# Pinning the gathered-row steps of a retrieval layer between the one-hots of its gate map

## The chip, the cores and the metric

The kernel runs on one core of a Trainium2 chip. The metric is device time in microseconds (us) of one launch, the median of several runs. The core's engines work through their own instruction lists in order: PE (matrix multiply), DVE (vector), ACT (activation), POOL (here the engine that issues gathers) and SP (here the engine that issues the other DMAs). An engine that waits for another one, or for a DMA, holds up everything behind it in its own list.

## The reference, cut to what matters

One decoder layer over 528 tokens: a mixing sub-layer (state-space scan and convolution), then the retrieval sub-layer that the change touches, then a final norm. The retrieval, per token:

```python
s1, s2 = q1 . sub_keys_1, q2 . sub_keys_2          # 8 heads, 128 scores each
v1, i1 = top_k(s1, 16);  v2, i2 = top_k(s2, 16)    # first top-k
top_s, pos = top_k(v1[:, None] + v2[None, :], 16)  # second top-k, over the 16*16 sums
expert = i1 * 128 + i2 at pos;  gate = softmax(top_s)
y = sum over 128 (head, k): gate * gelu(x . w_down[expert]) * w_up[expert]
```

There are 16384 experts with rows of 1024 float32 in `w_down` and in `w_up`. The input has 512 tokens that are kept.

## The kernel before, in words

The 512 tokens are four tiles of 128. Three of them are computed densely: all 16384 experts are multiplied with the 384 tokens, 128 experts at a time, and a gate map (a 128 x 128 table for each token, nonzero at its chosen experts) selects. The fourth tile is computed sparsely: for each of its 128 (head, k) pairs, one indirect DMA fetches 128 rows of `w_down` (512 KB), a DVE instruction multiplies them with the tokens and sums (L911), and the same is done with rows of `w_up` (L918, which adds gate times row to the output tile). That makes 256 steps, each a gather on POOL (L895) and a **use** on DVE (L911 or L918). They come out of a generator, 32 of `w_down`, then 32 of `w_up`, and so on. `pump(x)` adds x to a counter and takes as many steps as the counter's whole part.

The stages around the change, in the order of the program:

- `second(t)`, for the tiles 3, 0, 1, 2: the second top-k on DVE (many small instructions, lines 759 to 876). Tile 3 comes first, since the gathers need its expert numbers.
- `gate_map(n, b)`, 12 calls of 4 one-hot groups: each group builds four f16 one-hot tables of 128 x 1024 on DVE (L946, L947 and twice L949), 16 small matmuls on PE (L954, L955) combine them, and ACT copies the result out (L957). The one-hot tables are double-buffered.
- 86 **downs** `down(i, ...)`: 24 matmuls each (L160, L161, L162) of a 128-expert block of `w_down` with the 384 tokens. Each needs its weights split into two parts: ACT takes the high part (L754), DVE the low part (L755), and the third matmul of each triple (L162) reads what L755 wrote. There are 4 buffers for the parts. The downs are written after the map in the code, but with a higher priority (`early(AHP)`), so the build lays them between the second top-k and the map on all engines.
- The main loop over 128 blocks of `w_up`, 18 matmuls of 512 columns each, and from block 88 on with one more down in each pass. Here a use stands in each pass, later three.

The order on each engine is fixed when the kernel is built, by priorities and by an estimate of when things are ready. Gathers always keep their order of the program; a use keeps its place among the instructions that are written around it only where the list `paced` is not empty:

```python
    def use(r):
        if paced:
            tc.keep_in_program_order(r)
```

Before the main loop, gathered rows go to two buffers (`gat1`), so a gather waits on POOL until the use two steps earlier has ended. The main loop has six (`gat2`).

Of the kernel before, what the change touches and what calls it, by code (L numbers as in the profile page):

```python
# [35 lines left out]
LNP = 500  # L36
AHP = 1000
SPL = 0
SPRATE = (4.0, 1.03, 3.33, 0)
NQ = 2  # L40
NT = 4
HOLD = 2
# [75 lines left out]
def body(ctx, tc, I, out):  # L118
# [9 lines left out]
    def ps(tag="pb"):  # L128
        return psp.tile([128, 512], F32, name=tag, tag=tag)
# [4 lines left out]
    def late(n):  # L134
        return tc.high_priority(offset=-n)
# [17 lines left out]
    def load(dst, src):  # L153
        return nc.sync.dma_start(dst, src)
# [4 lines left out]
    def mm3(o, lh, ll, rh, rl, first, last):  # L159
        E.matmul(o, lh, rh, start=first, stop=False)  # L160
        E.matmul(o, lh, rl, start=False, stop=False)  # L161
        E.matmul(o, ll, rh, start=False, stop=last)  # L162
# [606 lines left out]
    def down(i, tag, ahead, leng):  # L769
        wh, wl = split_n(raw_n(I["wdT"][i].rearrange("p c j -> p (c j)"), 1024), 1024, leng)  # L770
        p = ps(tag)
        for dc in range(8):
            o = dc * 128
            mm3(p[:, :ND], wh[:, o:o + 128], wl[:, o:o + 128], hl(dc)[0][:, :ND], hl(dc)[1][:, :ND], dc == 0, dc == 7)
        hg = HG[hgn[0] % 6]
        hgn[0] += 1
        S.activation(hg, p[:, :ND], AF.Gelu)  # L777
        if ahead:
            load(HD[i], hg)
        else:  # L780
            HB[i] = hg
# [119 lines left out]
    paced = []  # L901
# [22 lines left out]
    def pump(x):  # L924
        spn[0] += x
        while spn[0] >= 1:
            spn[0] -= 1
            next(sp, None)

    for t in (3, 0, 1, 2):  # L930
        second(t)
        if t < 3:
            pump(SPRATE[3])

# [3 lines left out]
    def gate_map(n, b):  # L938
        gb = GBUF[n % 2]
        half = lambda a: a.rearrange("p t (j s) -> p t j s", s=2)  # L940
        io = iota16.rearrange("p (j s) -> p j s", s=2)[:, None].to_broadcast([128, TB, 64, 2])
        for q in range(GB // TB):
            t0 = GB * b + TB * q
            ob, oa = OB[q % 2], OA[q % 2]
            col = lambda a: a[:, t0:t0 + TB, None, :].to_broadcast([128, TB, 64, 2])
            V.tensor_tensor(half(ob), io, col(i2d), op=OP.is_equal)  # L946
            V.tensor_tensor(half(OE), io, col(i1d), op=OP.is_equal)  # L947
            for s in range(2):
                V.tensor_tensor(half(oa[s]), half(OE), col(gd[s]), op=OP.mult)  # L949
            for k0 in range(0, TB, 4):  # L950
                p = ps()
                for k in range(4):
                    po = p[:, 128 * k:128 * k + 128]
                    E.matmul(po, ob[:, k0 + k, :], oa[0][:, k0 + k, :], start=True, stop=False)  # L954
                    E.matmul(po, ob[:, k0 + k, :], oa[1][:, k0 + k, :], start=False, stop=True)  # L955
                c = TB * q + k0
                S.activation(gb.rearrange("p i t -> p t i")[:, c:c + 4, :], p.rearrange("p (t i) -> p t i", t=4),  # L957
                             AF.Copy, scale=1.0 / GS)
        for q in range(4 if n < NB - 2 else 0):
            load(GD[b, :, 32 * q:32 * q + 32, :], gb[:, 32 * q:32 * q + 32, :])  # L960

# [3 lines left out]
    def up_prep(i, leng):  # L965
        wh, wl = split_n(raw_n(I["wu"][128 * i:128 * i + 128, :], 1024), 1024, leng)
        if i not in HB:
            HB[i] = HG[hgn[0] % 6]
            hgn[0] += 1
            load(HB[i], HD[i])  # L970
        if i % 4 == 0:
            grt[i // 4] = GR[(i // 4) % 2]
            load(grt[i // 4], GD[:, :, i:i + 4, :].rearrange("b j i t -> j b i t"))
        gr = grt[i // 4]
        sf, sh, sl = SF[i % 2], SH[i % 2], SL[i % 2]
        if i >= 130 - NT:
            sh, sl = memr(R_U + 768 * (i % 2), 384), memr(R_U + 768 * (i % 2) + 384, 384)
        sf3, hb3 = [a.rearrange("p (b t) -> p b t", t=GB) for a in (sf, HB[i])]
        V.tensor_tensor(sf3[:, :NB - 2], hb3[:, :NB - 2], gr[:, :, i % 4, :], op=OP.mult)
        V.tensor_tensor(sf3[:, NB - 2:], hb3[:, NB - 2:], GLAST[:, :, GB * i:GB * i + GB], op=OP.mult)  # L980
        S.activation(sh, sf, AF.Copy)  # L981
        V.tensor_tensor(sl, sf, sh.bitcast(F32), op=OP.subtract)  # L982
        return sh, sl, wh, wl

    def up_mm(i, Y, ops, ms, hfs=(0, 1)):
        sh, sl, wh, wl = ops
        f, l = i == 0, i == 127
        for m in ms:
            c = slice(128 * m, 128 * m + 128)
            for hf in hfs:  # L990
                d = slice(512 * hf, 512 * hf + 512)
                mm3(Y[m][hf], sh[:, c], sl[:, c], wh[:, d], wl[:, d], f, l)

    for n in range(NB):
        gate_map(n, n if n < NB - 2 else 2 * NB - 3 - n)
        with late(SPL):
            pump(SPRATE[0])

    with early(AHP):
        for i in range(NQ, NAHEAD):  # L1000
# [1 line left out]

    ring[0] = gat2
    gn[0] = 0
    paced.append(True)
    ops = {}
    Y = [[ps("pa"), ps("pa")], [ps("pa"), ps("pa")], [ps(), ps()]]
    for i in range(128):
        for j in {127 - NT: range(128 - NT, 128)}.get(i, () if i > 127 - NT else (i + 1,)):
            if NAHEAD <= j < 128:  # L1010
                down(j, "pb", False, V)
        pump(0 if i < HOLD else SPRATE[1] if i < NAHEAD else SPRATE[2])
        ops[i] = up_prep(i, V)
# [48 lines left out]
```

## Time and profile before

| what | value |
|---|---|
| median of 3 runs | 1705.93 us (1703.87 to 1708.15) |
| the profiled execution: its own time, its span | 1709.63 us, 1707.9 us |
| PE busy, share of the span | 1643.6 us, 96% |
| DVE busy | 1397.6 us, 82% |
| ACT, POOL busy | 770.7 us, 397.6 us |
| second top-k with gathers, map and downs | about 637 to 1014 us |
| main loop | about 1014 to 1697 us |

The span is what the trace covers; all places below are us from its start. Busy time says how long an engine worked, not whether that work sets the end; for this one reads in a stretch which engine had idle time and whom it waited for.

### The profile page before, as it was taken

To read this page: it belongs to the slowest core of one execution; us is meant where nothing else is said; L and a number is where in the kernel's file an instruction comes from. 1 tells how busy PE (TensorE), PEld (TensorE's weight loads), DVE (VectorE), ACT (ScalarE), POOL (GpSimd) and SP (SyncE) were. 2 spreads that over 40 slices of the span, in tenths; PEclk is the share of its full clock that TensorE was granted. 3 is DMA by queue.
4 is the path that set the end of the run, shared out by engine and by line. 5 is a ranking of instruction groups with operands and counts; after the bars stand their busy time and mean duration, and the time that the engine had idled before them with its cause. 6 is when DMAs were issued, how large, how long until landed. Compare 5 with 4: busy or idle time off the path is not lost. (4 is left out here: it accounts for less than half of the span.)

```text
span 1707.9 us, 26157 instructions
## 1 busy us (share of the span) xinstructions
PE 1643.6 (96%) x9529; PEld 1487.2 (87%) x9529; DVE 1397.6 (82%) x2864; ACT 770.7 (45%) x1155; POOL 397.6 (23%) x336
## 2 busy tenths in 40 slices
PE   7999999799899999899999999999999999999997
PEld 7999999577788999898889988888888899999996
DVE  4998999974469998989889458888888889888885
ACT  5566554445333344356668533333333333333333
POOL 1111110110000003233410013222222254454540
PEclk9999999589999999999999999999999999999999
DMA  6877574454422458799888679999999899999892
GB/s 209 194 176 164 143 163 123 141 136 119 128 83 75 131 177 271 271 301 327 306 308 301 211 233 364 347 348 357 352 341 355 317 341 363 357 347 348 324 328 86
DMA packets 165185, 425.38 MB, mean 249 GB/s; under 512 B 14384, under 2 KB 81200, under 8 KB 159424
## 3 DMA queue, kind: packets, MB, share of 16 engines
q1 hardware_dynamic: 121568, 261.17, 43.8%
q0 software_dynamic: 43488, 162.55, 31.4%
q8 instruction: 74, 1.21, 0.3%
q14 instruction: 55, 0.45, 0.1%
HBM read 381.72 MB, written 41.94 MB: 248 GB/s over the span
## 5 line engine op out<-in xcount | busy, mean ns | idle before, releaser
L161 PE MATMUL pa<-MR 128*128 128x512 f32 (+3 forms) x2120 | 731.3, 345 | 3.4 <-DMA MR<-wout 3.4
L160 PE MATMUL pa<-MR 128*128 128x512 f32 (+3 forms) x2120 | 728.5, 345 | 6.1 <-ACT M L777 1.7
L162 PE MATMUL pa<-MR 128*128 128x512 f32 (+3 forms) x2120 | 693.8, 345 | 6.5 <-DVE MR L755 5.1
L160 PEld LDWEIGHTS pa<-MR 128*128 128x128 f32 x2120 | 405.2, 191 | 38.6 <-ACT M L777 2.3
L162 PEld LDWEIGHTS pa<-MR 128*128 128x128 f32 x2120 | 404.0, 191 | 38.3 <-DVE MR L755 5.4
L161 PEld LDWEIGHTS pa<-MR 128*128 128x128 f32 x2120 | 404.9, 191 | 34.9 <-DMA MR<-wout 4.6
L754 ACT ACTIVATE MR<-M 128x1024 fp32r<-128x1024 f32 (+1 forms) x264 | 285.8, 1083 | 307.1 <-PE pa L161 130.4
L755 DVE TENSOR_TENSOR MR<-M,MR 128x1024 fp32r<-128x1024 f32 (+1 forms) x264 | 330.0, 1251 | 97.4 <-ACT MR L754 96.5
L895 POOL DMA_INDIRECT M<-wu,M x128 | 177.7, 1388 | 387.4 <-DVE M L918 255.6
L895 POOL DMA_INDIRECT M<-wd,M x128 | 156.2, 1220 | 471.8 <-DVE M L911 209.6
L161 PE MATMUL pb<-MR 128*128 128x384 f32 (+1 forms) x576 | 206.6, 359 | 0.0
L160 PE MATMUL pb<-MR 128*128 128x384 f32 (+1 forms) x576 | 206.6, 359 | 0.0
L162 PE MATMUL pb<-MR 128*128 128x384 f32 (+1 forms) x576 | 205.0, 359 | 0.0
L981 ACT ACTIVATE MR<-M 128x384 fp32r<-128x384 f32 x128 | 67.0, 523 | 262.2 <-issue 202.9
L918 DVE SCALAR_TENSOR_TENSOR M<-M 128x1024 f32<-128x1024 f32 x128 | 163.5, 1278 | 15.4 <-DMA M<-wu,M 15.1
L422 DVE SCALAR_TENSOR_TENSOR M<-M 128x512 f32<-128x512 f32 x240 | 173.6, 743 | 2.6 <-ACT M L420 1.5
L911 DVE SCALAR_TENSOR_TENSOR M<-M 128x1024 f32<-128x1024 f32 x128 | 154.6, 1218 | 14.0 <-DMA M<-wd,M 13.7
L160 PEld LDWEIGHTS pb<-MR 128*128 128x128 f32 x576 | 108.1, 188 | 11.3
L161 PEld LDWEIGHTS pb<-MR 128*128 128x128 f32 x576 | 108.1, 188 | 11.2
L982 DVE TENSOR_TENSOR MR<-M,MR 128x384 fp32r<-128x384 f32 x128 | 71.0, 555 | 56.6 <-ACT MR L981 56.6
L162 PEld LDWEIGHTS pb<-MR 128*128 128x128 f32 x576 | 108.1, 188 | 10.4
L957 ACT ACTIVATE M<-pb 128x512 f32<-128x512 f32 x96 | 97.3, 1151 | 36.8 <-PE pb L955 35.2
(221 smaller groups left out, 1485.4 us busy)
## 6 DMA issues: line engine op xcount, KB each, us to landing
M<-wdT SPq DMA_DIRECT2D x128, 512.0 KB, 5.1
M<-wu SPq DMA_DIRECT2D x128, 512.0 KB, 6.5
GD<-M SPq DMA_DIRECT2D x40, 512.0 KB, 6.3
M<-GD SPq DMA_DIRECT2D x32, 640.0 KB, 7.6
M<-win SPq DMA_DIRECT2D x19, 1024.0 KB, 5.5
MR<-win POOLq DMA_DIRECT2D x38, 512.0 KB, 6.7
HD<-M SPq DMA_DIRECT2D x88, 192.0 KB, 4.3
M<-HD SPq DMA_DIRECT2D x88, 192.0 KB, 6.2
```

The source lines that it names most:

```text
L160: E.matmul(o, lh, rh, start=first, stop=False)
L161: E.matmul(o, lh, rl, start=False, stop=False)
L162: E.matmul(o, ll, rh, start=False, stop=last)
L422: V.scalar_tensor_tensor(o, gl[:, j:j + 512], cw[:, j:j + 1], o, op0=OP.mult, op1=OP.add)
L754: S.activation(wh, raw, AF.Copy)
L755: leng.tensor_tensor(wl, raw, wh.bitcast(F32), op=OP.subtract)
L895: r = G.indirect_dma_start(out=g, out_offset=None, in_=src, in_offset=bass.IndirectOffsetOnAxis(ap=e3[:, k:k + 1], axis=0))
L911: use(V.scalar_tensor_tensor(g, g, 1.0, x2s, op0=OP.mult, op1=OP.mult, accum_out=dots[:, k:k + 1]))
L918: use(V.scalar_tensor_tensor(h1[3], g, act3[:, k:k + 1], h1[3], op0=OP.mult, op1=OP.add))
L957: S.activation(gb.rearrange("p i t -> p t i")[:, c:c + 4, :], p.rearrange("p (t i) -> p t i", t=4), AF.Copy, scale=1.0 / GS)
L981: S.activation(sh, sf, AF.Copy)
L982: V.tensor_tensor(sl, sf, sh.bitcast(F32), op=OP.subtract)
```

## The change

Four numbers and three lines change. Before, four steps are pumped behind each of the 12 gate maps and their uses are not pinned. After, two steps are pumped behind the second top-k of each of the tiles 0, 1 and 2 (6, not pinned), three quarters of a step behind each of the 48 one-hot groups (36, pinned), and 6 behind the last gate map (pinned). Both make 48 steps ahead of the main loop. In the main loop a pass takes 1.0 step in place of 1.03 up to block 87, and 3.3 in place of 3.33 from there on.

```diff
-SPRATE = (4.0, 1.03, 3.33, 0)
+SPRATE = (3.0, 1.0, 3.3, 2, 6)
@@ in gate_map, in the loop over the 4 one-hot groups
                 S.activation(gb.rearrange("p i t -> p t i")[:, c:c + 4, :], p.rearrange("p (t i) -> p t i", t=4),
                              AF.Copy, scale=1.0 / GS)
+            pump(SPRATE[0] / 4)
@@ ahead of the main loop
+    paced.append(True)
     for n in range(NB):
         gate_map(n, n if n < NB - 2 else 2 * NB - 3 - n)
-        with late(SPL):
-            pump(SPRATE[0])
+    pump(SPRATE[4])
...
     ring[0] = gat2
     gn[0] = 0
-    paced.append(True)
```

The line that pumps behind a second top-k (`if t < 3: pump(SPRATE[3])`) is there before, with 0.

What this does to the order on DVE shows at three places. In the rows, L755 is the split for a down, L911 and L918 are uses, L946, L947 and L949 one-hots, the other lines small steps of the second top-k; "x2" means two in a row.

The first place is DVE in the second top-k, two rows behind the split for a down that the trace of before shows at 665.41 (rows 6). Before:

```order
L859 TENSOR_SCALAR M<-M 128x128
L911 SCALAR_TENSOR_TENSOR M<-M 128x1024
L860 TENSOR_TENSOR M<-M 128x256
L861 SCALAR_TENSOR_TENSOR M<-M 128x128
L832 TENSOR_TENSOR M<-M 128x2048
L755 TENSOR_TENSOR MR<-M,MR 128x1024
L911 SCALAR_TENSOR_TENSOR M<-M 128x1024
L834 TENSOR_TENSOR M<-M 128x2048
L862 TENSOR_SCALAR M<-M 128x128
L867 TENSOR_TENSOR M<-M 128x128
```

The same place after:

```order
L859 TENSOR_SCALAR M<-M 128x128
L860 TENSOR_TENSOR M<-M 128x256
L861 SCALAR_TENSOR_TENSOR M<-M 128x128
L832 TENSOR_TENSOR M<-M 128x2048
L834 TENSOR_TENSOR M<-M 128x2048
L755 TENSOR_TENSOR MR<-M,MR 128x1024
L862 TENSOR_SCALAR M<-M 128x128
L867 TENSOR_TENSOR M<-M 128x128
L838 TENSOR_TENSOR M<-M 128x1024
L947 TENSOR_TENSOR M<-M 128x1024
```

The uses are gone from here: from the split at 665.41 to the third split behind it (at 691.87 in rows 6) five uses stood before and none stands after, with the same steps of the second top-k between (but for one L873 and one L762, which now stand behind that split).

The second place is DVE in the midst of the map. Before:

```order
L918 SCALAR_TENSOR_TENSOR M<-M 128x1024
L947 TENSOR_TENSOR M<-M 128x1024
L755 TENSOR_TENSOR MR<-M,MR 128x1024
L949 TENSOR_TENSOR M<-M 128x1024 x2
L946 TENSOR_TENSOR M<-M 128x1024
L918 SCALAR_TENSOR_TENSOR M<-M 128x1024
L947 TENSOR_TENSOR M<-M 128x1024
L755 TENSOR_TENSOR MR<-M,MR 128x1024
L918 SCALAR_TENSOR_TENSOR M<-M 128x1024
```

After:

```order
L911 SCALAR_TENSOR_TENSOR M<-M 128x1024
L755 TENSOR_TENSOR MR<-M,MR 128x1024
L947 TENSOR_TENSOR M<-M 128x1024
L946 TENSOR_TENSOR M<-M 128x1024 x2
L949 TENSOR_TENSOR M<-M 128x1024 x2
L911 SCALAR_TENSOR_TENSOR M<-M 128x1024
L947 TENSOR_TENSOR M<-M 128x1024
L755 TENSOR_TENSOR MR<-M,MR 128x1024
L949 TENSOR_TENSOR M<-M 128x1024 x2
L911 SCALAR_TENSOR_TENSOR M<-M 128x1024
```

Here the uses now stand one behind each one-hot group, with a group between any two of them, and every fourth group has none; before, their distances are uneven. Both pieces run from one use to the second one behind it, which is the pair that shares a buffer.

The third place is DVE behind the last one-hots of the map. Before:

```order
L949 TENSOR_TENSOR M<-M 128x1024 x2
L755 TENSOR_TENSOR MR<-M,MR 128x1024 x10
L979 TENSOR_TENSOR M<-M 128x320
L980 TENSOR_TENSOR M<-M 128x64
L982 TENSOR_TENSOR MR<-M,MR 128x384
```

After (line numbers behind the map are one higher):

```order
L949 TENSOR_TENSOR M<-M 128x1024 x2
L918 SCALAR_TENSOR_TENSOR M<-M 128x1024
L755 TENSOR_TENSOR MR<-M,MR 128x1024
L918 SCALAR_TENSOR_TENSOR M<-M 128x1024
L755 TENSOR_TENSOR MR<-M,MR 128x1024
L918 SCALAR_TENSOR_TENSOR M<-M 128x1024
L755 TENSOR_TENSOR MR<-M,MR 128x1024
L918 SCALAR_TENSOR_TENSOR M<-M 128x1024 x2
L755 TENSOR_TENSOR MR<-M,MR 128x1024
L918 SCALAR_TENSOR_TENSOR M<-M 128x1024
L755 TENSOR_TENSOR MR<-M,MR 128x1024
L918 SCALAR_TENSOR_TENSOR M<-M 128x1024
```

Behind these follow seven more L755. Seven uses have come in between the last splits, where before there was none.

## Rows read from the trace of the kernel before

**Rows 1.** Page, part 1: busy us, share of the span, instructions.

```profile
PE 1643.6 (96%) x9529; PEld 1487.2 (87%) x9529; DVE 1397.6 (82%) x2864; ACT 770.7 (45%) x1155; POOL 397.6 (23%) x336
```

**Rows 2.** Waits of PE, 680 to 1000: total us, times, longest.

```profile
PE pb L954 <- DVE M L949: 8.3, 8, 2.5
PE pa L162 <- DVE MR L755: 5.1, 1, 5.1
PE pb L955 <- DVE M L949: 0.3, 1, 0.3
PE pa L160 <- ACT M L777: 0.3, 1, 0.3
```

**Rows 3.** Windows: length, then busy us of PE, PEld, DVE, ACT, POOL; PEclk, DMA share, GB/s.

```profile
697.00:699.00 2.00, 2.00 (x13) 2.00 (x12) 2.00 (x8) 0.00 (x0) 1.29 (x1) 0.92 0.98 350
836.00:838.00 2.00, 2.00 (x14) 1.84 (x13) 2.00 (x3) 2.00 (x4) 0.00 (x0) 0.68 0.77 283
```

**Rows 4.** Windows of 40 us: ahead of the main loop, and in it.

```profile
960.00:1000.00 40.00, 40.00 (x231) 39.74 (x230) 14.52 (x17) 15.10 (x22) 0.00 (x0) 1.00 0.65 215
1040.00:1080.00 40.00, 40.00 (x178) 33.12 (x177) 33.46 (x52) 14.75 (x20) 9.22 (x10) 1.00 1.01 366
```

**Rows 5.** Timeline of PE: start, duration, then idle before and its releaser.

```profile
654.96 0.33 PE L160 MATMUL pa<-MR 128*128 128x384 f32 x1
...
659.12 0.33 PE L160 MATMUL pa<-MR 128*128 128x384 f32 x1
...
693.17 0.69 PE L162 MATMUL pa<-MR 128*128 128x384 f32 x1 [5.12 <-DVE MR L755]
```

**Rows 6.** Timeline of DVE in the second top-k.

```profile
665.41 1.22 DVE L755 TENSOR_TENSOR MR<-M,MR 128x1024 fp32r<-128x1024 f32 x1
...
672.35 1.23 DVE L911 SCALAR_TENSOR_TENSOR M<-M 128x1024 f32<-128x1024 f32 x1 [0.99 <-DMA M<-wd,M]
...
691.87 1.25 DVE L755 TENSOR_TENSOR MR<-M,MR 128x1024 fp32r<-128x1024 f32 x1
```

**Rows 7.** Timeline of DVE in the map.

```profile
817.13 1.28 DVE L949 TENSOR_TENSOR M<-M 128x1024 f16<-128x1024 f16 x2
...
818.94 1.27 DVE L918 SCALAR_TENSOR_TENSOR M<-M 128x1024 f32<-128x1024 f32 x1
...
820.74 1.21 DVE L755 TENSOR_TENSOR MR<-M,MR 128x1024 fp32r<-128x1024 f32 x1
821.87 1.28 DVE L949 TENSOR_TENSOR M<-M 128x1024 f16<-128x1024 f16 x2
...
832.03 1.28 DVE L918 SCALAR_TENSOR_TENSOR M<-M 128x1024 f32<-128x1024 f32 x1 [5.34 <-DMA M<-wu,M]
...
856.96 1.28 DVE L918 SCALAR_TENSOR_TENSOR M<-M 128x1024 f32<-128x1024 f32 x1 [4.56 <-DMA M<-wu,M]
...
875.43 1.28 DVE L918 SCALAR_TENSOR_TENSOR M<-M 128x1024 f32<-128x1024 f32 x1 [2.84 <-DMA M<-wu,M]
```

**Rows 8.** Waits of DVE, 760 to 880, and of PE, 797 to 882.

```profile
DVE M L918 <- DMA M<-wu,M: 15.1, 6, 5.3
...
PE pb L954 <- DVE M L949: 6.2, 6, 2.5
```

**Rows 9.** Timeline of POOL: two gathers.

```profile
652.70 0.94 POOL L895 DMA_INDIRECT M<-wd,M  x1 [2.56 <-DVE M L911]
...
820.48 4.09 POOL L895 DMA_INDIRECT M<-wu,M  x1 [0.65 <-DVE M L918]
```

**Rows 10.** Gathers' issues, 760 to 880 and 880 to 960: median us to landing.

```profile
M<-wu,M POOLq DMA_INDIRECT x19, 8.1
...
M<-wu,M POOLq DMA_INDIRECT x3, 5.9
```

**Rows 11.** Timeline of DVE near the end of the main loop.

```profile
1675.19 1.23 DVE L755 TENSOR_TENSOR MR<-M,MR 128x1024 fp32r<-128x1024 f32 x1 [2.04 <-ACT MR L754]
...
1682.83 0.56 DVE L982 TENSOR_TENSOR MR<-M,MR 128x384 fp32r<-128x384 f32 x1 [2.31 <-ACT MR L981]
```

## The prediction, made blind

> **What bounds the kernel now.** Start with the busy times on the page: PE works for 96% of the span, DVE for 82% [rows 1]. So PE is the first candidate, and what a change can gain is what PE does not work. In the main loop it has nothing to give: in a window there PE is busy for all of its 40.00 us while DVE has 33.46 [rows 4], and so it goes on until PE's last matmul. Time that is saved or lost ahead of the main loop therefore reaches the end one for one.
>
> The change moves instructions between 637 and 1014 us, so the next view is whom PE waits for there. Four rows hold nearly all of it [rows 2]: one wait of 5.1 us for a split (L755), eight waits of 8.3 us in all and one of 0.3 for one-hots (L949), and 0.3 for ACT. DVE is thus the engine that is waited for, although it isn't the busiest. The waits cost twice where they are long, since PE runs at half clock for a while behind them. Behind the one that ended at 693.17 [rows 5] the granted clock is at its lower level of 1.2 GHz until about 697.3 (the mean of 0.92 in the stretch from 697 means 0.3 us of it at half [rows 3]): 4.1 us at half, so 2.1 lost. Behind the one at 834.0 it lasts until about 837.3 (0.68 in the stretch from 836 means 1.3 us at half): 3.3 us, so 1.6 lost. All that PE loses here is 5.1 + 0.3 + 2.1 = 7.5 us in the second top-k, and 8.3 + 0.3 + 1.6 = 10.2 in the map, 17.7 in all. That is the ceiling of a gain; work itself isn't removed on any engine.
>
> **The first place, the second top-k.** PE's wait of 5.12 us ended when the split that starts at 691.87 was done [rows 5, 6]. Five uses stand on DVE between the split at 665.41 and that one; after, none does. A use takes 1.23 us, 0.08 of it beside its successor (so 1.15), and one of the five waited 0.99 for its rows [rows 6]. The split comes 5 x 1.15 + 1.0 = 6.7 us sooner, and PE wants it 5.1 sooner. ACT's part of that down is done long before, so nothing else is late next. I count the whole 7.5 us; the bound from below is 0, if other steps of the top-k were as late.
>
> **The second place, the map.** The uses that left the second top-k now stand in the map, so DVE gets more to do there: 36 pinned uses instead of those 24 or so that the build had put into the first two thirds. What made PE wait in the map before is not DVE's work but its waiting: uses waited 15.1 us for their rows, six times [rows 8], 12.7 of it at 832.03, 856.96 and 875.43 [rows 7]. Behind a waiting use stand the one-hots that PE wants next. A gather can only start when the use two steps earlier has ended, so what counts is how much other work DVE has between a use and the second use behind it. I add it from the two excerpts of the order with steps of 1.13 us for a split, 0.60 for a one-hot and 1.20 for a use [rows 7]. Before, up to the use at 832.03: 0.60 + 1.13 + 1.20 + 0.60 + 1.20 + 0.60 + 1.13 = 6.5 us; up to the other two, added in the same way, 7.1 and 5.9. After, in the excerpt: 1.13 + 0.60 + 1.20 + 1.20 + 1.15 + 0.60 + 1.13 + 1.20 = 8.2 us. That is the close pair; two pairs of three have a further group in them and come to 10.6 or more.
>
> A gather lands 8.1 us after its issue (the median in the old map [rows 10]), and the issue comes 0.3 us behind the use's end (818.94 + 1.27 to 820.48 [rows 7, 9]): 8.4 us, just what the close pair has. The late ones still wait. If the gathers came as late as those that waited, the three long waits shrink at the close pairs by the added distance: 5.3 - 1.7 = 3.6, 4.6 - 1.1 = 3.5, 2.8 - 2.3 = 0.5, and the short ones (2.4 us in three) vanish: 7.6 us in 16 uses. Twelve uses of the 36 are such: 5.7 us. At the other 24, with 10.6, the long ones leave 1.2 + 1.1 = 2.3 in 16 uses: 3.4 us. DVE would wait some 9 us in the whole map. Of DVE's 15.1 before, PE felt 6.2 [rows 8], that is 0.41, since a finished group lies ready for it; so PE loses 9 x 0.41 = 3.7, and I take 4. The bounds are 0 (every gather at the median) and 36 x 6.2 / 16 = 14 (the old rate of waits at every use).
>
> One thing in the rows speaks against the change: a gather occupied POOL for 0.94 us beside a float32 split, and 4.09 beside f16 one-hots, a split and a use, and that gather was the one that landed at 832.03, 11.55 us after its issue [rows 7, 9]. The Trainium skill (SBUF — State Buffer, section "SBUF: two separate sides") says that DVE in a two-port mode holds the port pair that it shares with GpSimd, which then can't write the descriptors of its DMAs, so that the transfer seems blocked by DVE. By that rule the change would be bad at its core, since it puts all of the map's gathers next to one-hots; the trace agrees for the long gathers. Whatever the cause, the second rival below gives the time if all were so.
>
> **The third place, behind the map.** Seven uses now stand among the last splits, with only 2.3 to 5.3 us of work between a use and the second behind it, so they go at the pace of the gathers: two per landing and use. Landing takes 5.9 us there [rows 10] with 0.3 ahead of it, plus a use of 1.2: 7.4 for two, 26 us for seven. In that time DVE delivers five splits. PE takes 4.16 us for a down (654.96 to 659.12 [rows 5]), 6.25 downs, and with four buffers two to three splits lie ready. So I count nothing; DVE has the room later (14.52 us busy in 40 [rows 4]). Without that cover, at 11.8 us per landing, the seven take 45 us, PE could do 10.9 downs and has 7.5: 14 us lost. That is the other bound.
>
> **The rest.** In the main loop a use less in 33 passes, and 122 instead of 119.4 steps from block 88 on: the last use moves from pass 36 to pass 37 of those, one pass later. DVE has waits of 2.04 and 2.31 us there [rows 11] against one or two uses of 1.2, so nothing; up to 2 if they should not cover it. No DMA is added on SP, and the gathers pass nothing else on POOL.
>
> **The sum.** -7.5 - 10.2 + 4 = -13.7 us. The profiled execution took 1709.63 us with a span of 1707.9, so it would come to 1695.9 with a span of 1694.2. The median of the runs lies 3.7 below the profiled one, at 1705.93; the same step from there gives **1692.2 us**.
>
> **The rivals.** First, *the waits only move*: pinned uses wait for their rows at the old rate, 14 us lost in the map against 17.7 won, so -3.7: 1702. For it speaks that DVE has no less to do in all; against it the 8.2 us and more where 5.9 to 7.1 stood. Second, on the other side, *every gather in the map is as late as the one at 832.03*: 11.55 + 0.3 = 11.8 us. A gate map has one pair of 8.2 and two of 10.6: waits of 3.6 + 1.2 + 1.2 = 6.0, times 12 is 72 us on DVE, 0.41 of it 30 us on PE; 17.7 - 30 makes it 12 slower: 1718. It decides from the point where PE loses more than 17.7, that is 3.6 us of waits in a gate map, a landing 11.0 us behind a use. The median of 8.4 speaks against it; that the change sets every gather beside one-hots speaks for it. Third, *the seven uses starve PE*: +14 on the forecast, 1706, no change; the free DMA time there (0.65 of it used [rows 4]) speaks against it.
>
> **How the numbers follow.** From what a measurement of this kernel can tell, 0.3% (5.1 us), faster means under 1700.8. I give the forecast 0.70, the waits that only move 0.14, the third rival 0.08, the second 0.08. The forecast is faster, and a few of the first rival's cases too (0.02): faster 0.72. The rest of the first and most of the third are the same: 0.19. Slower: 0.09, the second and the worst of the third. The range begins at 1687, the whole 17.7 with a bit more of other waits, and ends at 1702, where the first rival lies; the others are left out. The forecast's own range is 1687 to 1698.
>
> **What would show it.** Right: PE doesn't wait at 688, the clock stays up there; PE's waits for one-hots sum to some 4 us instead of 8.6, DVE's for gathered rows in the map to under 12; PE has no wait between the last one-hot and the main loop; the main loop starts near 1000 instead of 1014. Wrong: gathers in the map that hold POOL for 3 to 4 us as a rule and land 11 us later; a wait of PE for a split behind the map; or idle time of PE in the main loop, which would mean that the saved time is lost later.

## The result, and the profile after

The changed kernel takes 1686.45 us (median of 4 runs, 1680.03 to 1686.92) against 1706.58 of the kernel before in the same comparison: a ratio of 0.9875, 95% interval 0.9848 to 0.9902. It is faster by 20.1 us; the forecast was 13.7, and the median lies 0.6 us below the low end of the range. The profiled execution has a time of 1686.24 us and a span of 1684.5.

The page of the kernel after, part 1 (against [rows 1]):

```profile
PE 1631.6 (97%) x9529; PEld 1477.1 (88%) x9529; DVE 1397.3 (83%) x2864; ACT 770.3 (46%) x1155; POOL 388.9 (23%) x336
```

No engine lost an instruction. PE has 12 us less of "busy" for the same work: 5.1 of it between the first gather and the main loop (345.4 and 340.2 us busy there), where the lower clock is gone, and 7.0 ahead of the first gather, where both kernels do the same. Whom PE waits for in the kernel after, from 640 to 1000 us (against [rows 2]):

```profile
engine line waited for: us in total, times, longest us
PE pb L880 <- DVE M L840: 1.9, 1, 1.9
PE pa L160 <- ACT M L777: 1.4, 1, 1.4
```

The wait of 5.1 us for a split in the second top-k and all nine waits for one-hots are gone. (L880 is a transpose of the second top-k, whose wait was 0.7 before; the one for L777, at 990.50, stands in the main loop.) Windows of the kernel after, the two short ones at the places of [rows 3] and the long one in the main loop as in [rows 4]; the columns are length, busy us of PE, PEld, DVE, ACT, POOL, then PE's granted clock, DMA share, GB/s:

```profile
697.00:699.00 2.00, 2.00 (x14) 2.00 (x13) 2.00 (x6) 1.17 (x3) 0.00 (x0) 1.00 0.98 258
836.00:838.00 2.00, 2.00 (x24) 1.84 (x22) 1.97 (x4) 1.43 (x2) 0.00 (x0) 1.00 1.01 414
...
1040.00:1080.00 40.00, 40.00 (x179) 33.10 (x178) 33.13 (x57) 14.75 (x20) 9.12 (x10) 1.00 0.98 356
```

The granted clock stays at its upper level where it was 0.92 and 0.68, and the main loop is as full of PE as before. So the gain lies ahead of the main loop. To measure it free of what happens earlier, take the time from the first gather to the first matmul of 512 columns, the first one of the main loop. (A few downs still stand behind it; the 1014 us given above as the start of the main loop is where those end, and after the change that is 990.5.) The two rows of the kernel before (timelines of POOL and of PE):

```profile
637.04 1.08 POOL L895 DMA_INDIRECT M<-wd,M  x1 [173.41 <-DVE M L876]
...
997.36 0.63 PE L160 MATMUL pb<-MR 128*128 128x512 f32 x2
```

and of the kernel after:

```profile
631.75 1.08 POOL L895 DMA_INDIRECT M<-wd,M  x1 [174.47 <-DVE M L876]
...
973.84 0.63 PE L160 MATMUL pb<-MR 128*128 128x512 f32 x2
```

This **stretch** is 997.36 - 637.04 = 360.3 us before and 342.1 after: 18.2 us. The gain is the same by the other mark (1014.02 - 637.04 against 990.50 - 631.75), and from the first 512-column matmul to PE's last one both kernels take 701.4 to 701.5 us. Every experiment below is read by the stretch. It is a fair measure only where it holds the same work: in four of the experiments (the added work in both forms, four at once with four buffers, nineteen uses) it holds 29 to 39 more of the downs' matmuls than the 1667 of the others, because the order at its end moved. The first gather's own start moved by 5.3 us too, but every instruction ahead of it stands in the same order in both kernels, and in the fourteen traces of this study it lies between 627 and 637 us whatever the kernel. That is scatter of the earlier stages; it is one reason why medians of a few runs differ by some us, and why the stretch is the better measure where its work is the same.

DVE's waits in the kernel after, from 700 to 910 us (in the map) and from 910 to 1000 (behind it), first rows of each:

```profile
DVE M L911 <- DMA M<-wd,M: 6.6, 6, 1.9
DVE M L918 <- DMA M<-wu,M: 2.8, 2, 1.7
```

```profile
DVE MR L755 <- ACT MR L754: 19.7, 7, 5.4
DVE M L918 <- DMA M<-wu,M: 11.6, 6, 2.6
```

DVE still waits 9.4 us for gathered rows in the map, where the forecast had 9, and 11.6 behind it. PE has no wait for one-hots or for a split beside either. Of the signs that the prediction named for being right, all came but two sizes: PE's waits for one-hots sum to 0 and not 4 us, and the main loop starts at 990.5 and not near 1000. That is the point to explain.

### The profile page after: what moved, and what is told of

It reads as the page before. It is cut to its first block, busy times and chain, and to the rows that moved or that the text cites. A ratio compares the mean times of both kernels' runs of the same rounds, so it can differ in the third digit from the quotient of the medians.

```text
span 1684.5 us, 26131 instructions
## 1 busy us (share of the span) xinstructions
PE 1631.6 (97%) x9529; PEld 1477.1 (88%) x9529; DVE 1397.3 (83%) x2864; ACT 770.3 (46%) x1155; POOL 388.9 (23%) x336
## 5 line engine op out<-in xcount | busy, mean ns | idle before, releaser
L755 DVE TENSOR_TENSOR MR<-M,MR 128x1024 fp32r<-128x1024 f32 (+1 forms) x264 | 330.5, 1253 | 81.5 <-ACT MR L754 77.1
L895 POOL DMA_INDIRECT M<-wu,M x128 | 167.2, 1306 | 310.6 <-DVE M L918 264.6
L982 ACT ACTIVATE MR<-M 128x384 fp32r<-128x384 f32 x128 | 67.0, 524 | 274.2 <-issue 203.2
L918 DVE SCALAR_TENSOR_TENSOR M<-M 128x1024 f32<-128x1024 f32 x128 | 163.8, 1279 | 14.6 <-DMA M<-wu,M 14.4
L911 DVE SCALAR_TENSOR_TENSOR M<-M 128x1024 f32<-128x1024 f32 x128 | 154.2, 1219 | 11.9 <-DMA M<-wd,M 11.9
L160 PEld LDWEIGHTS pb<-MR 128*128 128x128 f32 x576 | 108.1, 188 | 11.4
```

The lines of the kernel that those rows point to most:

```text
L755: leng.tensor_tensor(wl, raw, wh.bitcast(F32), op=OP.subtract)
L895: r = G.indirect_dma_start(out=g, out_offset=None, in_=src, in_offset=bass.IndirectOffsetOnAxis(ap=e3[:, k:k + 1], axis=0))
L911: use(V.scalar_tensor_tensor(g, g, 1.0, x2s, op0=OP.mult, op1=OP.mult, accum_out=dots[:, k:k + 1]))
L918: use(V.scalar_tensor_tensor(h1[3], g, act3[:, k:k + 1], h1[3], op0=OP.mult, op1=OP.add))
```

## The experiments

All names of lines are those of the kernel after; the stretch is worked out as above from each kernel's own two rows.

**The pin alone taken away.** The new numbers, but uses not pinned before the main loop.

```diff
-    paced.append(True)
     for n in range(NB):
         gate_map(n, n if n < NB - 2 else 2 * NB - 3 - n)
     pump(SPRATE[4])
...
+    paced.append(True)
```

> The pumps stand where the change puts them, but uses are pinned only from the main loop on, as before. The build then lays 24 uses into the second top-k and 24 into the first half of the map again, as before. My theory (pinning moves the uses, and their place is what PE loses by): the time of before, 1704 to 1708 us, with PE waiting about 5 us for a split near 688 and about 8.6 us for one-hots. Rival (the gain comes from the pumps' places in the code or from the main loop's rates of 1.0 and 3.3): near 1686.

1707.13 us, ratio 1.0015 (0.9999 to 1.0032), stretch 361.7. The build lays the uses exactly as before, and PE's waits are back:

```profile
PE pb L954 <- DVE M L949: 7.5, 7, 2.5
PE pa L162 <- DVE MR L755: 5.3, 1, 5.3
```

So the new numbers do nothing without the order that the pin fixes.

**The second top-k filled again.** Eight steps behind each of three second top-k calls in place of two, fewer in the map (24 uses and 17, in place of 7 and 34), all of the map's still pinned.

```diff
-SPRATE = (3.0, 1.0, 3.3, 2, 6)
+SPRATE = (1.5, 1.0, 3.3, 8, 6)
```

> Rates 1.5, 1.0, 3.3, 8, 6: 24 uses in the second top-k and the first one-hots as before, but only 17 in the rest of the map, 17 us of DVE work apart, 7 behind it. My theory (the two places cost separately): the top-k costs its 7.5 us again and the map nothing, so 1692 to 1696, with PE's wait of about 5 us for a split and none for one-hots. Rival (all of the gain comes from the map): 1686. Rival (all of it from the top-k): 1700 or more.

1698.71 us, ratio 0.9951 (0.9932 to 0.9969), stretch 354.6: above the 1692 to 1696 of my theory. PE's waits from 640 to 1000, and two windows, in the top-k and in the map:

```profile
PE pa L162 <- DVE MR L755: 6.1, 1, 6.1
PE pb L880 <- DVE M L840: 4.0, 3, 2.8
...
680.00:720.00 40.00, 33.54 (x182) 32.83 (x181) 37.62 (x115) 13.89 (x20) 10.15 (x10) 0.91 0.83 275
...
800.00:840.00 40.00, 40.00 (x333) 37.60 (x332) 37.52 (x55) 29.88 (x37) 7.15 (x4) 1.00 0.89 318
```

This separates the two places in one direction. With uses in the top-k, the wait for the split and the lower clock return there, and nowhere else. Of the 18.2 us, 12.5 are lost again, more than the 7.5 that the prediction gave this place, because this order has more of the L880 waits as well, with 3.4 us at the lower clock behind the longest of them; the map, which has half as many uses here as after the change, has no wait for one-hots. The other direction, an empty top-k with the long waits back in the map, was not run.

**One use behind every group.** All steps into the map: two uses ahead of it, 42 in it.

```diff
-SPRATE = (3.0, 1.0, 3.3, 2, 6)
+SPRATE = (4.0, 1.0, 3.3, 0, 0)
```

> Rates 4.0, 1.0, 3.3, 0, 0: none in the top-k, one pinned use behind each one-hot group, 48 in all, 4 of them behind the last. Pairs have 6 to 11 us of DVE work between them, much as in the changed kernel, but DVE's work in a gate map grows from 17.0 to 18.2 us against 17.7 of PE. My theory (PE feels waits for rows only where DVE has no slack left): PE waits for one-hots again, 5 to 20 us, so 1691 to 1706. Rival (number and waits do not reach PE as long as no pair is close): 1685 to 1688.

1683.88 us, ratio 0.9875 (0.9849 to 0.9902), stretch 340.6. PE has no wait at all in the stretch. My theory, that PE waits again once DVE has more work in a gate map than PE, fell: DVE's waits for rows from 700 to 910 sum to 0.9 us, and PE's for one-hots to nothing.

**Three buffers.** The kernel after with three buffers for gathered rows in the map, so that a gather can start one use earlier.

```diff
+    ring[0] = gat2[:3]
+    gn[0] = 0
     for n in range(NB):
         gate_map(n, n if n < NB - 2 else 2 * NB - 3 - n)
```

> The changed kernel with three buffers for gathered rows from the map on, so a gather starts one use earlier. DVE's waits for rows in the map (9.3 us in the changed kernel) and behind it (11.6) should vanish. My theory (PE does not feel these waits): no change, 1685 to 1688. Rival (0.4 of DVE's waits reach PE, as in my prediction): 3 to 4 us faster, 1682 to 1683.

1681.84 us, ratio 0.9870 (0.9849 to 0.9891), stretch 340.4. DVE's waits for rows from 700 to 910 are gone altogether, and the stretch is 1.7 us shorter than in the kernel after, in which the one wait for L840 alone is 1.9. Taking away the 9.4 us of waits gave PE nothing in the map, where it had no wait to lose. The median is 4.6 us below that of the kernel after, which is the rival's number and not the theory's; but the intervals of the two ratios lie over each other, and the trace shows 1.7 us of it in the stretch, none in the map.

**The change once more, and both variants together** (four steps per gate map and three buffers), in five rounds:

```diff
-SPRATE = (3.0, 1.0, 3.3, 2, 6)
+SPRATE = (4.0, 1.0, 3.3, 0, 0)
...
+    ring[0] = gat2[:3]
+    gn[0] = 0
```

> The changed kernel itself once more, in five rounds beside the kernel before. Theory: all that the change gains lies between the first gather and the main loop, where the traces show 360.3 us before and 342.1 after, so 18.2 us and a ratio near 0.989, and what stood beyond that in the first comparison (20 us, 0.9875) is the scatter of the stage ahead of it, which is the same code in both. Rival: the change also gains 2 us or more ahead of the first gather or in the main loop, and the ratio stays at 0.9875 or below.

> Three buffers and a use behind every group together, in five rounds. Both alone took PE's last wait (1.9 us for a down's input) out of the second top-k and came to 340.4 and 340.6 us between the first gather and the main loop, against 342.1 of the changed kernel; PE has nothing left to lose there, so together they give the same 340.5, and 1 to 2 us less than the changed kernel. Rival: uses land sooner still and DVE's room shows elsewhere: 4 us or more below the changed kernel.

The change: 1686.31 us, ratio 0.9882 (0.9861 to 0.9903), stretch 340.8. Both: 1684.53, ratio 0.9874 (0.9856 to 0.9891), stretch 341.5. The change gains 20.2 us by its medians and 18 to 21 by the stretch (360.3 and 361.7 in the old order, 342.1 and 340.8 in the new). The intervals contain both answers, so whether 1 or 2 us come from elsewhere stays open. No variant is shown to beat the change. (L880, which the second expectation calls a down's input, is a transpose of the second top-k.) Both together still have one wait of DVE of 4.00 us, and PE felt 0.4 of it (DVE, then PE):

```profile
705.34 1.23 DVE L911 SCALAR_TENSOR_TENSOR M<-M 128x1024 f32<-128x1024 f32 x1 [4.00 <-DMA M<-wd,M]
...
707.83 0.29 PE L954 MATMUL pb<-M 128*128 128x128 f16 x2 [0.36 <-DVE M L946]
```

**Added work on DVE, in two places or in sixteen.** A one-hot written again, 16 extra instructions in each kernel: eight at each of two groups (the first added line), or one at each of sixteen (the second, in the other kernel).

```diff
-            V.tensor_tensor(half(OE), io, col(i1d), op=OP.is_equal)
+            for _ in range(1 + 8 * (((n, q) in ((3, 0), (8, 1))))): V.tensor_tensor(half(OE), io, col(i1d), op=OP.is_equal)
...
+            for _ in range(1 + 1 * ((2 <= n < 10 and q % 2 > 0))): V.tensor_tensor(half(OE), io, col(i1d), op=OP.is_equal)
```

> The changed kernel with 5.5 us of added work on DVE at each of two places of the map (a one-hot written eight more times), 11 us in all. Theory of the lead: the one-hots are done some 2.3 us ahead of PE there, and a stall costs PE what is beyond that, 2 x (5.5 - 2.3) = 6.4 us, and 1.6 us of half clock behind each, so some 8 to 10 us more between the first gather and the main loop than the 342.1 of the changed kernel, with waits for one-hots (L949) at both places. Rival 1, the fixed share of the forecast: 0.41 of 11, 4.5 us. Rival 2, DVE's room alone counts: 11 us less what DVE has idle there, the same as with sixteen small ones.

> The same added work on DVE, 11 us, as sixteen pieces of 0.69 us in sixteen groups of eight gate maps (every second group's one-hot written once more). Theory of the lead: each piece is below the 2.3 us that the one-hots are ahead and DVE has some 9 us idle in the map to catch up with, so PE loses 0 to 3 us against the 342.1 of the changed kernel. Rival 1, the fixed share: 4.5 us as with the two large ones. Rival 2, DVE's room alone counts: the same loss as with the two large ones.

1691.53 us (ratio 0.9906, 0.9888 to 0.9924), stretch 351.2; and 1690.95 us (0.9916, 0.9892 to 0.9939), stretch 349.7. Neither had a wait for one-hots, not even beside a delay of 5.5 us. PE's waits with the two large ones, then with the sixteen:

```profile
PE pa L160 <- ACT MR L982: 4.6, 1, 4.6
PE pa L160 <- ACT M L777: 1.4, 1, 1.4
```

```profile
PE pa L160 <- ACT MR L982: 2.4, 1, 2.4
```

The test doesn't tell size from sum. The build knows the added instructions and lays other work of PE, downs, ahead of the late one-hots: in front of the first delayed group PE does 722 matmuls of downs instead of 670. What is missing then shows at the end of the stage, where PE's first matmul of the main loop waits for L982 (on ACT, L981 in the kernel before). The stretch holds 29 and 31 more matmuls here, some 5 us of PE's work, so it overstates the loss. From the first gather to the end of the span it takes 1059.5 and 1056.6 us, against 1052.7 and 1051.5 in the two traces of the changed kernel, and the medians are 5.2 and 4.6 above the 1686.31 of the changed kernel in the same comparison. That is near the 4.5 of the fixed share in both forms, though not by its path, as PE has no wait for one-hots; so this pair doesn't refute a share of added work.

**Four uses at once behind each gate map, pinned,** with two buffers, and then with four:

```diff
-SPRATE = (3.0, 1.0, 3.3, 2, 6)
+SPRATE = (4.0, 1.0, 3.3, 0, 0)
...
-            pump(SPRATE[0] / 4)
...
+    ring[0] = gat2[:4]
+    gn[0] = 0
     for n in range(NB):
         gate_map(n, n if n < NB - 2 else 2 * NB - 3 - n)
-    pump(SPRATE[4])
+        pump(SPRATE[0])
```

The `ring` and `gn` lines are in the second kernel only.

> The uses pinned as after the change, but four at once behind each gate map in place of three quarters behind each group: half of them stand 5.3 to 7.1 us of DVE's work behind the second use before, as in the kernel before. Theory (the distance matters, the pin alone does nothing): a gather lands 8.4 us behind a use, so two uses in a gate map wait some 2 to 3 us, some 50 us of DVE's waits for rows over the map where the changed kernel has 9 to 16, DVE's room of some 9 us is used up, and PE waits for one-hots again: 15 us or more over the 342 between the first gather and the main loop, a time of 1700 or more. Rival 1 (the pin alone does it): 340 to 343 us and 1686. Rival 2 (the fixed share of 0.41): 20 us.

> The same four at once behind each gate map, with four buffers for gathered rows in place of two, so that a gather can start a gate map (some 20 us) ahead of its use. Theory: uses no longer wait (DVE's waits for rows in the map under 4 us), and PE has no wait for one-hots: 340 to 342 us between the first gather and the main loop, 1683 to 1687. Rival: four uses in a row (4.8 us) by themselves hold up the one-hots beyond PE's 2 to 3 us of lead: 2 us a gate map, 24 us lost.

Two buffers: 1687.89 us, ratio 0.9911 (0.9890 to 0.9933), stretch 344.4. Four: 1680.94, ratio 0.9879 (0.9849 to 0.9909), stretch 344.3, with 8.0 us of DVE's waits for rows left from 700 to 910 and 0.2 us of PE's for one-hots, so four uses at once don't cost PE the 24 us of the rival; the theory's bound of 4 us of DVE's waits fell. I had expected 1700 or more of the first one, from DVE work of 5.3 to 7.1 us between paired uses and gathers that land 8.4 us behind. DVE's waits for rows from 700 to 910 were 7.3 us, not 50, and PE's for one-hots from 640 to 960:

```profile
PE pb L954 <- DVE M L949: 1.4, 2, 1.1
PE pb L955 <- DVE M L949: 0.3, 1, 0.3
```

So short distances alone don't make long waits: 14 of the 37 uses there had 5.3 to 7.1 us of DVE's work behind the second use before. What the expectation had wrong is the landing: the rows that were waited for were taken 5.6 to 7.7 us after their gather's start, not 8.1. Pricing by distance with one landing time for all gathers, as in the prediction's second place, is refuted; that distance counts is not.

**Nineteen uses behind the map** in place of seven:

```diff
-SPRATE = (3.0, 1.0, 3.3, 2, 6)
+SPRATE = (2.0, 1.0, 3.3, 2, 18)
```

> Nineteen uses behind the last one-hots in place of seven, and half a step in place of three quarters behind each group. The traces of the changed kernel show intervals of 4.1 us of such uses, so nineteen take some 78 us, in which PE works off its downs. Theory (third place at nothing as long as DVE's splits between the uses keep up with PE's downs of 4.16 us): with one split or so between two uses the pace is the same as PE's, and the gain stays, 340 to 345 us, 1684 to 1690. Rival (the other bound of the prediction): splits come at 5 in 26 us, 15 in 78 us, where PE could do 18.7 downs with 2 to 3 ready: PE loses 5 to 15 us, with waits for L755 behind the last one-hots.

1703.67 us, ratio 0.9990 (0.9971 to 1.0008), stretch 363.0 with 31 more matmuls in it: all of the gain is lost, and my theory with it. PE's waits from 900 to 1000, and DVE's for rows:

```profile
PE pa L162 <- DVE MR L755: 7.9, 3, 4.5
PE pa L160 <- ACT MR L982: 6.5, 1, 6.5
```

```profile
DVE M L918 <- DMA M<-wu,M: 32.9, 11, 4.2
...
DVE M L911 <- DMA M<-wd,M: 6.5, 1, 6.5
```

The third rival's mechanism exists; seven uses are just not enough for it.

**Nothing pinned, but four buffers.** The kernel before, with its own numbers:

```diff
+    ring[0] = gat2[:4]
+    gn[0] = 0
     for n in range(NB):
         gate_map(n, n if n < NB - 2 else 2 * NB - 3 - n)
         with late(SPL):
             pump(SPRATE[0])
```

> The kernel before with nothing pinned and its old numbers, but four buffers for gathered rows from the first gate map on. With them the build itself lays the uses elsewhere: two in place of some twenty-four stand in the second top-k, the others are spread over the map and its end. Theory: what counts is where the uses stand and that they do not wait long, not the pin; PE has no wait of 5 us in the top-k and DVE's waits for rows in the map stay under 3 us each, so 340 to 343 us between the first gather and the main loop, as after the change, and 1681 to 1687. Rival 1: without the pin the map's waits for one-hots (L949) come back, 8 us and half clock, 350 us and 1692 to 1696. Rival 2: nothing is gained without the pin, 360 us and 1705.

1683.20 us, ratio 0.9871 (0.9851 to 0.9891), stretch 340.8. With four buffers the build puts two uses in the top-k and the rest into the map by itself. DVE's waits for rows from 700 to 910 and PE's waits from 640 to 1000:

```profile
DVE M L911 <- DMA M<-wd,M: 18.8, 10, 3.7
...
DVE M L918 <- DMA M<-wu,M: 2.7, 2, 1.6
```

```profile
PE pb L954 <- DVE M L946: 2.3, 2, 1.8
```

The pin is one way to the order, not the cause of the gain. And 21.5 us of waits on DVE cost PE 2.3 here, where much the same sum, 23.6 from 700 to 910, cost 8.6 before.

## Why the prediction was right in direction and too small

**The ceiling held, with a bit more.** Of the waits that the prediction sums to "17.7 in all" none is left, and the stretch shortened by 18.2 in the first pair of traces (the wait for L840 grew by 1.2; some 1.7 more are in no row that I can name). That only time ahead of the main loop counts held too; the main loop is as full as before.

**The first place held.** The split comes in time and the wait for L755 is gone; with the uses put back the wait returns as 6.1 us. Its size is confirmed only roughly, since that kernel loses 12.5 in an order of its own.

**The step that failed is the +4 in the second place:** "Of DVE's 15.1 before, PE felt 6.2 [rows 8], that is 0.41, since a finished group lies ready for it; so PE loses 9 x 0.41 = 3.7, and I take 4." PE lost 0 there. The 9 came out (9.4 measured) partly by luck: the prediction had 5.7 of it at the close pairs and 3.4 at the others, and all of the 9.4 lies at pairs with 7.2 to 8.4 us of work, whose rows were taken 8.0 to 9.9 us after the gather's start. The factor was no constant. PE's waits for one-hots against DVE's waits for rows were 8.6 of 23.6 before, 0 of 9.4 after, 0 of 4.1 in the repeat, 2.3 of 21.5 with four buffers and no pin. Without the charge the sum is -17.7, that is 1688.2, inside the interval of both comparisons; the first median lies 1.8 us below it.

What one wait costs depends on how far its one-hots stand ahead of PE at that moment. In the kernel after, the longest wait in the map is followed like this (timeline of DVE, then of PE):

```profile
811.96 1.23 DVE L911 SCALAR_TENSOR_TENSOR M<-M 128x1024 f32<-128x1024 f32 x1 [1.94 <-DMA M<-wd,M]
...
815.45 1.28 DVE L949 TENSOR_TENSOR M<-M 128x1024 f16<-128x1024 f16 x2
...
817.77 0.29 PE L954 MATMUL pb<-M 128*128 128x128 f16 x2
```

The group that was delayed was finished at 815.45 + 1.28 = 816.73 and PE took it up at 817.77: 1.0 us of the wait's cover was left. Before, the wait of 5.34 us that ended at 832.03 [rows 7] was longer than its cover, which was 5.34 - 2.52 = 2.8:

```profile
833.97 0.39 PE L954 MATMUL pb<-M 128*128 128x128 f16 x2 [2.52 <-DVE M L949]
```

A factor from the sum of waits hides this. Nor is the cover one number, and short waits close together add up: in both variants together 4.00 us cost 0.4, while before the change a wait of 2.16, with waits of 0.78 and 0.56 in the 9 us ahead of it, was followed by one of 1.18 on PE:

```profile
766.16 1.23 DVE L911 SCALAR_TENSOR_TENSOR M<-M 128x1024 f32<-128x1024 f32 x1 [2.16 <-DMA M<-wd,M]
...
769.79 0.28 PE L954 MATMUL pb<-M 128*128 128x128 f16 x2 [1.18 <-DVE M L949]
```

That is read from the traces; the experiment made to show it by itself (two delays or sixteen) did not separate the two, so the size of the cover isn't shown by a dose.

**The reason given for the long waits was half of it.** The prediction put them down to DVE work of 6 to 7 us between paired uses. With 14 of 37 uses at such distances, pinned, the longest wait for rows from 700 to 910 was 1.7 us. What the longest waits of the old order have in common besides is their gather. In the second trace of the old order (no pin), POOL's timeline, then DVE's:

```profile
813.47 4.09 POOL L895 DMA_INDIRECT M<-wu,M  x1 [0.65 <-DVE M L918]
...
838.52 4.09 POOL L895 DMA_INDIRECT M<-wu,M  x1 [0.65 <-DVE M L918]
```

```profile
824.96 1.28 DVE L918 SCALAR_TENSOR_TENSOR M<-M 128x1024 f32<-128x1024 f32 x1 [5.25 <-DMA M<-wu,M]
...
849.92 1.28 DVE L918 SCALAR_TENSOR_TENSOR M<-M 128x1024 f32<-128x1024 f32 x1 [4.59 <-DMA M<-wu,M]
```

Both waits over 4 us belong to gathers that held POOL for 4.09 us and whose rows were used 11.4 us after their start, as with the one at 832.03 in [rows 7, 9]. (The third long one before, 2.84 us at 875.43, is of another kind: its gather held POOL for 1.15 us.) A held gather alone makes no long wait either. The three held ones in the map of the kernel after had 7.2, 12.0 and 10.2 us of DVE's work to hide in, and their uses waited 1.0, 0 and 0 us. With four uses at once and two buffers, a gather held as long, with 7.2 us of work, made a wait of 1.1 (POOL, then DVE):

```profile
904.00 4.09 POOL L895 DMA_INDIRECT M<-wu,M  x1 [0.66 <-DVE M L918]
...
912.90 1.28 DVE L918 SCALAR_TENSOR_TENSOR M<-M 128x1024 f32<-128x1024 f32 x1 [1.14 <-DMA M<-wu,M]
```

All gathers from 725 to 930 us, before and then after (groups of POOL: count, busy, mean ns):

```profile
L895 POOL DMA_INDIRECT M<-wu,M x19 | 40.1, 2113 | 66.0 <-DVE M L918 51.0 <-DVE M L911 7.7 <-DMA M<-wu,M 7.0
L895 POOL DMA_INDIRECT M<-wd,M x13 | 16.8, 1291 | 36.7 <-DVE M L911 29.3 <-DVE M L870 4.8 <-DVE M L840 2.7
```

```profile
L895 POOL DMA_INDIRECT M<-wd,M x21 | 29.2, 1391 | 98.7 <-DVE M L911 98.7
L895 POOL DMA_INDIRECT M<-wu,M x14 | 26.9, 1920 | 54.3 <-DVE M L918 44.6 <-DVE M L911 9.7
```

The long ones are all gathers of `w_up`: seven of 2.8 us or more before, three after, none among those of `w_down` in either. The change takes 17 uses out of the top-k, so its map begins with the 25 steps of `w_down` that are left, and has fewer of `w_up`. The pairs in its map stand further apart too. Which of the two shortened the long waits, and by how much, is not shown; no run exchanged the kinds alone.

**The second rival** would have made the change slower if every gather in the map were held up. They were not: beside one-hots most hold POOL for 1.1 to 1.7 us. The held one at 820.48 was released inside a float32 instruction: 820.48 + 4.09 = 824.57 is 0.89 us into the use at 823.68 that follows three one-hots in a row. The Trainium skill (SBUF — State Buffer, section "SBUF: two separate sides") has DVE and GpSimd share one pair of ports as an exclusive lock, which a DVE instruction holds in a two-port mode or, against a GpSimd instruction that reads SBUF, with two inputs from SBUF. The long holds agree with some such lock, but a gather of `w_down` beside a run of five one-hots took 1.68 us (802.05 in the kernel after), which that alone doesn't explain. The prediction took the one-hots to be in such a mode; no run here shows in which mode they ran.

**The third place** held for seven uses: they came every 4.2 us (918.70 to 943.77 for six intervals is 4.18), where the forecast had 26 / 7 = 3.7, and PE's downs had cover. At nineteen it costs all that was won.

**The rest** at nothing held: the 701.4 and 701.5 us behind the stretch.

**The range** began at 1687 because only the ceiling's "bit more" stood below 1688. The ceiling itself was summed from four wait rows and two stretches of lower clock, and the profiled start of the stretch moves by several us from one execution to the next; neither had a place in the range. So the charge of 4 put the forecast too high, and the missing scatter put the low end of the range too high; with the charge at nothing and the same low end the median would still lie 0.6 us outside.

## What to carry to other kernels

Price a wait by its own length against how far the finished work stands ahead of the engine that wants it, not by a share of the sum of waits. Look for the few long waits and ask what their transfers have in common; a distance prices a wait only together with the landing time of that very transfer. When most of a gain is the removal of waits, let the range reach below the ceiling by the scatter of the stages that were not changed.

## What was not expected of the hardware

A gather's time on POOL went with the table that it read: in the map, gathers of `w_down` stayed at or under 1.7 us in both kernels, those of `w_up` reached 4.09 beside one-hots and splits of the same kinds. The uses beside them differ too (L911 and L918), so whether the table or the use matters, and why, is open. And an order with uses four at a time and four buffers, 344.3 us in the stretch, still came to 1680.94, since part of PE's work, 39 matmuls, had only moved across the mark at its end.
